# Dense gates of an expert mixer: three bf16 products for one float32 product, and other products in the warm-up

## Chip, core and metric

One core of one Trainium2 chip runs the whole program. The metric is device time in microseconds (us), the median of three runs.

## What is computed

A decoder trunk of two layers over 256 tokens of width 1024, all float32. Each layer has an attention mixer and then an expert mixer; a last RMSNorm ends it. The change lies in the expert mixer, which the reference computes so (cut; 16384 experts are the pairs of 128 first and 128 second indices, 8 heads pick 16 each):

```
q = (t @ w_query).reshape(T, PEER_HEADS, 2, PEER_HALF)
s = jnp.einsum('thpd,pnd->thpn', q, sub_keys)
top_s, top_i = lax.top_k(s, PEER_TOPK)
...
experts = jnp.take_along_axis(cand_i, best_pos, axis=-1).reshape(T, PEER_HEADS * PEER_TOPK)
gates = jax.nn.softmax(best_s, axis=-1).reshape(T, PEER_HEADS * PEER_TOPK)
...
act = jax.nn.gelu(jnp.einsum('td,ted->te', tb, expert_u[eb]), approximate=False)
out = jnp.einsum('te,ted->td', gb * act, expert_v[eb])
```

## The kernel before

The kernel gathers no experts. It multiplies the tokens by all rows of `expert_u` and sums over all rows of `expert_v`, with gates that are zero where an expert was not picked. Weights come in blocks of 128 x 1024 float32, in the order of use; each is split into two float32r parts, `hi` by ScalarE (ACT, L90) and `lo` by VectorE (DVE, L91), up to two blocks ahead, and every product of such operands is three matmuls on TensorE (PE): high by high, high by low, low by high (L119 to L121 for 256 columns, L152 for 512). SP issues the loads (L110).

The program runs layer by layer: the norm (`inv_rms`, `norm_t`), the mixer, the norm again, then `peer`. In `peer` 16 blocks give the queries and their scores; `select` finds the picked pairs and their gates on DVE while the first 48 chunks of `expert_u` are multiplied (a chunk is one of 128 blocks, that is one second index; 24 matmuls of 256 columns). At its end the indices and the gates are transposed to `tT`, with the pick along the partitions and the token along the columns (L942 on PE, L945 on ACT).

Then comes the dense stage: 65 rounds, b = 0 to 64, over blocks of four tokens (`TB`), with the last 80 chunks spread over them. A round with one chunk is called short here, one with two long. A round does, in the order written by hand and kept on each engine:

- `one_hots(b+1)`: DVE compares a table of indices, `iotax`, with the tokens' picks, for the first and the second index: two bf16 tiles [pick, index, token] (L761);
- `proj`: the next chunk (with the split of a later block on ACT and DVE);
- `gated(b+1)`: ACT scales the second index's rows by the gate, token by token, into float32 `ohG` (L770), and copies the first's into float32 `oh` (L771);
- `apply(b-1)`: DVE multiplies the finished chunks by the gates of block b-1 (L786, L788), ACT stores the gates for the later ones (L790);
- `dense(b)`: for each of the four tokens one float32 product of [pick, first index] and [pick, gated second index], 128 x 128, into PSUM (L779);
- for the chunk, ACT's gelu (L743, L745) and DVE's product with gates already stored (L747).

After it, 128 blocks of `expert_v` follow with 12 matmuls of 512 columns each (L152).

At the start PE runs 14 float32 products of a tile `ones` (L285) until the tokens are there. The norm's squares on ACT (L214) write their unused results over `hT[0]`; a diagonal with the reciprocal root (L243) then transposes and scales the tokens on PE (L246), and ACT and DVE cut the result into `hT[0]` and `hT[1]` (L251, L252).

Of the kernel before, what the change touches and what calls it, by code (L numbers as in the profile page):

```python
# [22 lines left out]
S = 256  # L23
# [12 lines left out]
WARM = 14  # L36
# [9 lines left out]
class Kern:  # L46
# [26 lines left out]
    def weights(self, *key):  # L73
        """The two float32r parts of the next block."""
        n = self.used
        self.used += 1
        assert self.blocks[n][0] == key, (self.blocks[n][0], key)
        self.ahead(n + 3)
        return self.split[n]

    def ahead(self, n):
        """Splits blocks up to the n-th and fetches more."""
        nc = self.nc
        while len(self.split) < min(n, self.limit, len(self.blocks)):
            if len(self.raws) == len(self.split):
                self.fetch()
            raw, w = self.raws[len(self.split)]
            hi = self.ring(self.stream, "hi", [128, D + 8], F32R, 3)
            lo = self.ring(self.stream, "lo", [128, D + 8], F32R, 3)
            nc.scalar.activation(hi[:, :w], raw[:, :w], AF.Copy)  # L90
            nc.vector.tensor_sub(lo[:, :w], raw[:, :w], hi[:, :w].bitcast(F32))  # L91
            self.split.append((hi, lo))
        while len(self.raws) < min(len(self.split) + RAWS, len(self.blocks)):
            self.fetch()
# [28 lines left out]
    def proj(self, *key, tag="ps"):  # L123
        """[128 columns, tokens] of h times a block of weights."""
        w = self.by_k(self.weights(*key))
        ps = self.bank(tag)[:, :S]
        self.mm3(ps, [((w[0][:, k], w[1][:, k]), (self.hT[0][:, k], self.hT[1][:, k])) for k in KO])
        return ps

    def ring(self, pool, name, shape, dtype, n):  # L130
        """The next of n tiles that take turns."""
        key = (id(pool), name, *shape)
        if key not in self.rings:
            self.rings[key] = [[pool.tile(shape, dtype, name=f"{name}{q}") for q in range(n)], 0, pool]
        r = self.rings[key]
        while True:
            r[1] += 1
            t = r[0][(r[1] - 1) % n]
            if not any(t is h for h in self.held):
                return t  # L140
# [4 lines left out]
    def rows_b(self, accs, lhs, w, tt, width, first, last):  # L145
        """accs[g] += lhs^T rows (128 of the contraction) times a natural block of weights."""
        hi, lo = w
        lh = lhs[0][..., tt * 128:(tt + 1) * 128]
        ll = lhs[1][..., tt * 128:(tt + 1) * 128]
        for n, (a, b) in enumerate(((lh, hi), (lh, lo), (ll, hi))):  # L150
            for g, ps in enumerate(accs):
                self.nc.tensor.matmul(ps[:, :width], a, b[:, g * width:(g + 1) * width],  # L152
                                      start=first and n == 0, stop=last and n == 2)

    def sum_b(self, n, key, lhs_of):
        """x += sum of n blocks; the last blocks run piece by piece of the result, so that the norm starts early."""
# [26 lines left out]
    def rsqrt_end(self, pool, vy):  # L183
        """One Newton step on the power, in two parts; gives -2 / sqrt."""
# [12 lines left out]
    def inv_rms(self, also=lambda n: None):  # L197
        """Generator: finishes the sums into x; gives -2 / rms of the rows of the first tile of tokens, then of the
        second; also(n) goes with the n-th piece."""
# [35 lines left out]
    def norm_t(self, pool, g):  # L235
        """hT = transpose of the normed x, as two float32r parts; g: the gains [128, KT]. The transposing product
        with a diagonal applies 1 / rms."""
# [18 lines left out]
    def build(self):  # L256
        nc, tc, i = self.nc, self.tc, self.i
        with ExitStack() as st:
# [21 lines left out]
            # the tensor engine's clock rises with work: it runs on ones until x is there  # L280
            ones = const.tile([128, 128], F32, name="ones")
            nc.vector.memset(ones, 1.0)
            ps = self.bank("ps")
            for _ in range(WARM):
                nc.tensor.matmul(ps[:, 0:128], ones, ones, start=True, stop=True)  # L285
            self.iotab = const.tile([128, TOPK], BF, name="iotab")
            self.iotax = const.tile([128, 128, TB], BF, name="iotax")
            self.starts = const.tile([128, 2, 16], BF, name="starts")
# [27 lines left out]
    def constants(self, pool):  # L316
        """Generator, in three steps: the bias by distance (negated) and the mask, over all pairs of tokens, into DRAM."""
# [23 lines left out]
        # the rows run against the distance: read them upside down, turn them with a permutation  # L341
# [12 lines left out]
    def mixer(self, l):  # L354
        nc, tc, i = self.nc, self.tc, self.i
        lam_init = 0.8 - 0.6 * math.exp(-0.3 * l)
        with tc.tile_pool(name="mix", bufs=1) as mp, tc.tile_pool(name="att", bufs=1) as ap, ExitStack() as first:
            self.norm_t(ap, self.gains[:, 0, l])
            # small operands
# [15 lines left out]
            # values and forget logits  # L375
# [26 lines left out]
            # operands of the forgetting scores: even heads in rows 0..63 with their decay in rows 64..79,  # L402
            # odd heads in rows 64..127 with their decay in rows 0..15
# [56 lines left out]
            # branch projections, merge  # L460
# [41 lines left out]
    def forget(self, mp, psv, bf, tri, sel, fq, fk):  # L502
        """Generator, in eight steps: decay operands of the forgetting heads."""
# [8 lines left out]
        # -log_sigmoid(z) = max(-z, 0) + log1p(exp(-|z|))  # L512
# [30 lines left out]
    def exps(self, ap, ps, tb, sums):  # L543
        """exp of the logits less their maximum, both tiles of queries; ps holds the negated scores, tb the
        negated bias."""
# [13 lines left out]
    def turn(self, ap, w):  # L559
        """Transposed weights as blocks (keys 0, queries 0), (keys 0, queries 1), (keys 1, queries 1)."""  # L560
        nc = self.nc
        pt = self.bank("ps")
        for q in range(3):
            nc.tensor.transpose(pt[:, q * 128:(q + 1) * 128], w[:, q * 128:(q + 1) * 128], self.ident)  # L564
        wt = self.ring(ap, "wt", [128, 384], F32, 3)
        nc.scalar.activation(wt, pt[:, 0:384], AF.Copy)
        return wt

    def diff_head(self, ap, h, qk, tb, nlam, dv, ydT, gsub):
        """Generator, in seven steps of one block of weights each: a differential head."""  # L570
# [51 lines left out]
    def fox_pair(self, ap, c, fq, fk, tb, dv, yfT):  # L622
        """Generator, in four steps: two forgetting heads."""
# [34 lines left out]
    def peer(self, l):  # L658
        nc, tc, i = self.nc, self.tc, self.i
        with ExitStack() as st:  # L660
            sm = st.enter_context(tc.tile_pool(name="sm", bufs=1))
            pa = st.enter_context(tc.tile_pool(name="bufa", bufs=1))
            tT = [sm.tile([128, S], F32 if q == 2 else BF, name=f"tT{q}") for q in range(3)]
# [51 lines left out]
            with tc.tile_pool(name="wp", bufs=1) as wp:  # L715
                # dense gates, token by token, against the chunks so far; the later chunks take them as they come
# [37 lines left out]
    def one_hots(self, sm, b, tT):  # L754
        """Rows of the first and of the second index for some tokens, [index, token]."""
# [3 lines left out]
        o = [self.ring(sm, "ohb", shp, BF, 2) for _ in range(2)]  # L759
# [4 lines left out]
    def gated(self, sm, b, tT, hot):  # L764
        """The rows token by token in float32, those of the second index scaled by the gates."""
        nc = self.nc
        oa = self.ring(sm, "oh", [128, TB, 128], F32, 2)
        og = self.ring(sm, "ohG", [128, TB, 128], F32, 2)
        for t in range(TB):
            nc.scalar.activation(og[:, t], hot[1][:, :, t], AF.Copy, scale=tT[2][:, b * TB + t:b * TB + t + 1])  # L770
        nc.scalar.activation(oa, hot[0].rearrange("p n t -> p t n"), AF.Copy)  # L771
        return oa, og

    def dense(self, hots):
        """Gates of all experts [first index, second index] for some tokens."""
        oa, og = hots
        ps = self.bank("acc").rearrange("p (t c) -> p t c", c=128)
        for t in range(TB):
            self.nc.tensor.matmul(ps[:, t], oa[:, t], og[:, t], start=True, stop=True)  # L779
# [12 lines left out]
    def score(self, tk, sk, q, u):  # L792
        """Scores of one half-head against its sub-keys."""
# [8 lines left out]
    def top16(self, tk, items, tag):  # L802
        """Generator: the largest 16 of each list, in order, and their places; the lists take turns."""
# [14 lines left out]
    def select(self, tk, tT):  # L818
        """Best 16 of each half-head, best 16 sums of each head, their experts and gates; yields the time
        that each piece takes on the vector engine, in microseconds, or None to let the other engines catch up."""  # L820
# [29 lines left out]
        # gates; places and index lists as bf16 (whole numbers below 128)  # L850
# [14 lines left out]
        by_h = lambda t: t.rearrange("p (h k) r -> p h k r", h=PH)  # noqa: E731  # L865
# [23 lines left out]
        # row of the candidates: as many as start at or before the place; column: the place less the row's start  # L889
# [15 lines left out]
        # first index: sum of the steps up to the row  # L905
# [17 lines left out]
        # second index: the one at the column  # L923
# [14 lines left out]
        for tt in both:  # L938
# [5 lines left out]
            for q in range(3):  # L944
                nc.scalar.activation(tT[q][:, tt * 128:(tt + 1) * 128], ps[:, q * 128:(q + 1) * 128], AF.Copy)  # L945


def lay_out(inputs, depth=2):
    """Inputs as the kernel reads them: rearranged, never changed."""
# [26 lines left out]
def shape_constants():  # L976
# [9 lines left out]
    # row p < 8 carries ones against the keys' sums, rows 8..15 the queries' sums against ones  # L986
# [11 lines left out]
    # bucket of distance 255 - n; the last row is the mask  # L998
# [27 lines left out]
```

## Time and profile before

| what | value |
|---|---|
| median of three runs | 2064.69 us (2063.64 to 2064.99) |
| profiled execution, first to last instruction (its span; the page gives no other time for it) | 2062.4 us |
| mean granted clock of TensorE | 0.999 of full |
| PE, DVE, ACT busy | 99%, 66%, 63% of the span |

The profile shows one execution. Matmuls are pipelined and their ends are modelled, so a listed duration reaches into the next matmul; distances between starts tell the rate. A weight load (PEld) overlaps the matmul before it. A float32 matmul of the program appears as two records.

### The profile page before, as it was taken

To read this page: it belongs to the slowest core of one execution; us is meant where nothing else is said; L and a number is where in the kernel's file an instruction comes from. 1 tells how busy PE (TensorE), PEld (TensorE's weight loads), DVE (VectorE), ACT (ScalarE), POOL (GpSimd) and SP (SyncE) were. 2 spreads that over 40 slices of the span, in tenths; PEclk is the share of its full clock that TensorE was granted. 3 is DMA by queue.
4 is the path that set the end of the run, shared out by engine and by line. 5 is a ranking of instruction groups with operands and counts; after the bars stand their busy time and mean duration, and the time that the engine had idled before them with its cause. 6 is when DMAs were issued, how large, how long until landed. Compare 5 with 4: busy or idle time off the path is not lost.

```text
span 2062.4 us, 36624 instructions
## 1 busy us (share of the span) xinstructions
PE 2046.8 (99%) x14052; PEld 1888.7 (92%) x14052; DVE 1363.1 (66%) x2990; ACT 1290.6 (63%) x2600; POOL 28.0 (1%) x50
## 2 busy tenths in 40 slices
PE   9999999999999999999999999999999999999998
PEld 8998999999999888888899989999999998888886
DVE  5667798666677555555566668985666775555555
ACT  6666446688888444444466655467888874444444
POOL 2000000000000000000010000000000000000000
PEclk9999999999999999999999999999999999999999
DMA  7445565544444555656554455665444546565654
GB/s 229 148 154 167 164 184 177 181 149 149 148 150 148 182 192 186 192 186 192 186 171 146 157 172 159 190 187 171 145 154 144 152 145 193 186 192 186 191 185 153
DMA packets 97392, 352.72 MB, mean 171 GB/s; under 512 B 11152, under 2 KB 11317, under 8 KB 97216
## 3 DMA queue, kind: packets, MB, share of 16 engines
q1 hardware_dynamic: 95472, 345.68, 53.9%
q0 software_dynamic: 1456, 4.18, 0.7%
q8 instruction: 110, 1.80, 0.4%
q14 instruction: 66, 0.54, 0.1%
q10 hardware_dynamic: 288, 0.52, 0.1%
HBM read 348.62 MB, written 1.71 MB: 170 GB/s over the span
## 4 chain that ended last, share of the span: by engine, by line
PE 98%; issue 1%; DMA 0%; POOL 0%; DVE 0%; ACT 0%; POOLq 0%; SPq 0%
PE acc L152 37%; PE ps L120 17%; PE ps L119 17%; PE ps L121 17%; PE acc L779 6%; PE ps L152 1%; PE acc L797 1%; PE acc L246 1%; PE acc L634 1%; PE ps L564 0%; PE acc L576 0%; DMA tr<-erow 0%; PE acc L651 0%; DMA x<-x 0%; PE acc L120 0%
## 5 line engine op out<-in xcount | busy, mean ns | idle before, releaser
L91 DVE TENSOR_TENSOR lo<-raw,hi 128x1024 fp32r<-128x1024 f32 (+1 forms) x656 | 801.9, 1224 | 497.9 <-ACT hi L90 493.4
L90 ACT ACTIVATE hi<-raw 128x1024 fp32r<-128x1024 f32 (+1 forms) x656 | 694.8, 1060 | 395.3 <-PE acc L152 387.9
L119 PE MATMUL ps<-hT,hi 128*128 128x256 f32 x2784 | 799.6, 287 | 0.0
L120 PE MATMUL ps<-hT,hi 128*128 128x256 f32 x2784 | 784.5, 282 | 0.0
L121 PE MATMUL ps<-hT,lo 128*128 128x256 f32 x2784 | 779.0, 280 | 0.0
L152 PE MATMUL acc<-hi,cut 128*128 128x512 f32 x2048 | 561.1, 395 | 0.0
L119 PEld LDWEIGHTS ps<-hT,hi 128*128 128x128 f32 x2784 | 523.4, 188 | 3.9 <-issue 3.7
L121 PEld LDWEIGHTS ps<-hT,lo 128*128 128x128 f32 x2784 | 525.1, 189 | 0.0
L120 PEld LDWEIGHTS ps<-hT,hi 128*128 128x128 f32 x2784 | 523.6, 188 | 0.3
L152 PEld LDWEIGHTS acc<-hi,cut 128*128 128x128 f32 x2048 | 385.4, 188 | 90.0
L152 PE MATMUL acc<-lo,cut 128*128 128x512 f32 x1024 | 321.9, 394 | 0.0
L152 PEld LDWEIGHTS acc<-lo,cut 128*128 128x128 f32 x1024 | 192.4, 188 | 45.8
L770 ACT ACTIVATE ohG<-ohb,tT 128x128 f32<-128x128 bf16 x512 | 168.6, 404 | 5.4 <-DVE ohb L761 2.2
L779 PE MATMUL acc<-ohG,oh 128*128 128x128 f32 x1024 | 134.7, 274 | 0.0
L747 DVE TENSOR_TENSOR bufb<-bufb,g 128x4 f32<-128x4 f32 (+25 forms) x156 | 45.9, 294 | 124.0 <-ACT g L743 124.0
L779 PEld LDWEIGHTS acc<-ohG,oh 128*128 128x128 f32 x1024 | 125.2, 191 | 0.0
L682 ACT ACTIVATE bufa<-ps 128x256 f32<-128x256 f32 x96 | 36.9, 384 | 115.7 <-PE ps L121 115.6
L761 DVE TENSOR_TENSOR ohb<-iotax,tT 128x512 bf16<-128x512 bf16 x256 | 96.5, 419 | 3.8 <-ACT oh L771 3.8
L743 ACT ACTIVATE g<-ps 128x4 f32<-128x4 f32 (+25 forms) x156 | 43.1, 276 | 75.5 <-PE ps L121 73.6
L771 ACT ACTIVATE oh<-ohb 128x512 f32<-128x512 bf16 x128 | 85.0, 664 | 0.0
L708 DVE TENSOR_TENSOR cut<-bufb,cut 128x256 fp32r<-128x256 f32 x160 | 67.1, 419 | 0.0
L707 ACT ACTIVATE cut<-bufb 128x256 fp32r<-128x256 f32 x160 | 64.0, 400 | 0.0
(235 smaller groups left out, 1442.8 us busy)
## 6 DMA issues: line engine op xcount, KB each, us to landing
raw<-uT SPq DMA_DIRECT2D x256, 512.0 KB, 3.5
raw<-expert_v SPq DMA_DIRECT2D x256, 512.0 KB, 4.3
raw<-wA SPq DMA_DIRECT2D x64, 512.0 KB, 3.7
raw<-wQ SPq DMA_DIRECT2D x32, 512.0 KB, 3.6
raw<-wV SPq DMA_DIRECT2D x16, 516.0 KB, 4.5
raw<-wO SPq DMA_DIRECT2D x16, 512.0 KB, 3.7
raw<-w_out SPq DMA_DIRECT2D x16, 512.0 KB, 4.3
tb<-table POOLq DMA_DIRECT2D x2, 640.0 KB, 5.6
```

Of the source, the lines that this page charges most:

```text
L90: nc.scalar.activation(hi[:, :w], raw[:, :w], AF.Copy)
L91: nc.vector.tensor_sub(lo[:, :w], raw[:, :w], hi[:, :w].bitcast(F32))
L119: self.nc.tensor.matmul(ps, ah, bh, start=first and q == 0, stop=False)
L120: self.nc.tensor.matmul(ps, ah, bl, start=False, stop=False)
L121: self.nc.tensor.matmul(ps, al, bh, start=False, stop=last and q == n - 1)
L152: self.nc.tensor.matmul(ps[:, :width], a, b[:, g * width:(g + 1) * width], start=first and n == 0, stop=last and n == 2)
L707: nc.scalar.activation(a[:, 0], chunk(n), AF.Copy)
L708: nc.vector.tensor_sub(a[:, 1], chunk(n), a[:, 0].bitcast(F32))
L761: nc.vector.tensor_tensor(o[q], self.iotax, tT[q][:, None, ts].to_broadcast(shp), op=OP.is_equal)
L770: nc.scalar.activation(og[:, t], hot[1][:, :, t], AF.Copy, scale=tT[2][:, b * TB + t:b * TB + t + 1])
L771: nc.scalar.activation(oa, hot[0].rearrange("p n t -> p t n"), AF.Copy)
L779: self.nc.tensor.matmul(ps[:, t], oa[:, t], og[:, t], start=True, stop=True)
```

## The change

The gates are no longer float32 in `tT[2]`. `select` cuts them into three bf16 parts, each the rounding of what the parts before leave, so that their sum is the gate exactly; the tile `gp` holds them [pick, part, token]. `gated` is now one DVE multiplication of the second index's one-hots with the three parts, into a bf16 tile [pick, part, index, token]; the first index's one-hots go to PE as they are, in a ring of two tiles (the second's have one). `dense` does three bf16 products per token into the same PSUM region. PE reads both operands with a step of four elements, since the token is the innermost dimension. ACT has no part in `gated` any more.

The warm-up is seven kinds of products, five times each: bf16 with 512, 128, 128 (both operands with a step of four) and 384 columns, float32r with 512, 512 (step of two) and 128 columns. The bf16 ones read `iotax`, set to ones; the float32r ones read the first half of `hT[0]`, set to ones. The tile `ones` is gone. The rest of the diff (left out) takes comments away.

```diff
-WARM = 14
+WARM = 5
...
-            ones = const.tile([128, 128], F32, name="ones")
-            nc.vector.memset(ones, 1.0)
-            ps = self.bank("ps")
-            for _ in range(WARM):
-                nc.tensor.matmul(ps[:, 0:128], ones, ones, start=True, stop=True)
             self.iotab = const.tile([128, TOPK], BF, name="iotab")
             self.iotax = const.tile([128, 128, TB], BF, name="iotax")
+            ones = self.hT[0][:, 0:4].rearrange("p k t -> p (k t)")
+            nc.vector.memset(self.iotax, 1.0)
+            nc.vector.memset(ones.bitcast(F32), 1.0)
+            ps = self.bank("ps")
+            onesb = self.iotax.rearrange("p n t -> p (n t)")
+            for a, b, n in ((onesb, onesb, 512), (onesb, onesb, 128), (self.iotax[:, :, 0], self.iotax[:, :, 1], 128),
+                            (onesb, onesb, 384), (ones, ones, 512), (ones, ones[:, ::2], 512), (ones, ones, 128)):
+                for _ in range(WARM):
+                    nc.tensor.matmul(ps[:, :n], a[:, 0:128], b[:, :n], start=True, stop=True)
...
-            tT = [sm.tile([128, S], F32 if q == 2 else BF, name=f"tT{q}") for q in range(3)]
+            tT = [sm.tile([128, S], BF, name=f"tT{q}") for q in range(2)] + [sm.tile([128, 3, S], BF, name="gp")]
...
-        o = [self.ring(sm, "ohb", shp, BF, 2) for _ in range(2)]
+        o = [self.ring(sm, f"oh{q}", shp, BF, 2 - q) for q in range(2)]
...
     def gated(self, sm, b, tT, hot):
-        nc = self.nc
-        oa = self.ring(sm, "oh", [128, TB, 128], F32, 2)
-        og = self.ring(sm, "ohG", [128, TB, 128], F32, 2)
-        for t in range(TB):
-            nc.scalar.activation(og[:, t], hot[1][:, :, t], AF.Copy, scale=tT[2][:, b * TB + t:b * TB + t + 1])
-        nc.scalar.activation(oa, hot[0].rearrange("p n t -> p t n"), AF.Copy)
-        return oa, og
+        og = self.ring(sm, "ohG", [128, 3, 128, TB], BF, 2)
+        shp = [128, 3, 128, TB]
+        self.nc.vector.tensor_tensor(og, hot[1][:, None].to_broadcast(shp),
+                                     tT[2][:, :, None, b * TB:(b + 1) * TB].to_broadcast(shp), op=OP.mult)
+        return hot[0], og
...
         for t in range(TB):
-            self.nc.tensor.matmul(ps[:, t], oa[:, t], og[:, t], start=True, stop=True)
+            for k in range(3):
+                self.nc.tensor.matmul(ps[:, t], oa[:, :, t], og[:, k, :, t], start=k == 0, stop=k == 2)
...
-            for q in range(3):
-                nc.scalar.activation(tT[q][:, tt * 128:(tt + 1) * 128], ps[:, q * 128:(q + 1) * 128], AF.Copy)
+            ts = slice(tt * 128, (tt + 1) * 128)
+            for q in range(2):
+                nc.scalar.activation(tT[q][:, ts], ps[:, q * 128:(q + 1) * 128], AF.Copy)
+            rest = self.ring(tk, "rest", [128, 128], F32, 2)
+            nc.scalar.activation(tT[2][:, 0, ts], ps[:, 256:384], AF.Copy)
+            nc.vector.tensor_sub(rest, ps[:, 256:384], tT[2][:, 0, ts])
+            nc.scalar.activation(tT[2][:, 1, ts], rest, AF.Copy)
+            nc.vector.tensor_sub(tT[2][:, 2, ts], rest, tT[2][:, 1, ts])
```

## Rows read from the trace of the kernel before

**Rows 1.** The page, busy time, share and instructions of each engine

```profile
PE 2046.8 (99%) x14052; PEld 1888.7 (92%) x14052; DVE 1363.1 (66%) x2990; ACT 1290.6 (63%) x2600; POOL 28.0 (1%) x50
```

**Rows 2.** The page, chain that ended last, shares by engine

```profile
PE 98%; issue 1%; DMA 0%; POOL 0%; DVE 0%; ACT 0%; POOLq 0%; SPq 0%
```

**Rows 3.** The same chain in order of time: start, length, engine, tile, line

```profile
395.08 0.89 PE acc L779 x8
401.65 0.89 PE acc L779 x8
405.37 0.89 PE acc L779 x8
```

**Rows 4.** Timeline of ACT, two chunks before the dense stage: start, length

```profile
386.62 0.38 ACT L682 ACTIVATE bufa<-ps 128x256 f32<-128x256 f32 x1 [0.99 <-PE ps L121]
...
389.45 0.38 ACT L682 ACTIVATE bufa<-ps 128x256 f32<-128x256 f32 x1 [1.49 <-PE ps L121]
```

**Rows 5.** Timeline of ACT, two blocks of expert_v

```profile
840.74 1.06 ACT L90 ACTIVATE hi<-raw 128x1024 fp32r<-128x1024 f32 x1 [1.41 <-PE acc L152]
...
843.53 1.06 ACT L90 ACTIVATE hi<-raw 128x1024 fp32r<-128x1024 f32 x1 [1.43 <-PE acc L152]
```

**Rows 6.** Window: PE, PEld, DVE, ACT, POOL busy, granted clock, DMA

```profile
394.00:672.00 278.00, 278.00 (x2384) 278.00 (x2383) 191.93 (x407) 236.16 (x612) 0.00 (x0) 1.00 0.49 150
```

**Rows 7.** Groups of weight loads, shapes apart: busy us, mean ns

```profile
L120 PEld LDWEIGHTS ps<-hT,hi 128*128 128x128 f32 x2784 | 523.6, 188 | 0.3
...
L564 PEld LDWEIGHTS ps<-ident,lg 128*128 128x128 f32 x48 | 5.4, 140 | 0.0
...
L333 PEld LDWEIGHTS acc<-oh,rel 33*5 33x5 f32 x2 | 0.1, 82 | 0.2 <-issue 0.2
```

**Rows 8.** Groups of ACT and DVE, shapes apart

```profile
L770 ACT ACTIVATE ohG<-ohb,tT 128x128 f32<-128x128 bf16 x512 | 168.6, 404 | 5.4 <-DVE ohb L761 2.2
...
L761 DVE TENSOR_TENSOR ohb<-iotax,tT 128x512 bf16<-128x512 bf16 x256 | 96.5, 419 | 3.8 <-ACT oh L771 3.8
...
L891 DVE TENSOR_TENSOR cmp<-wide,starts 128x2048 bf16<-128x2048 bf16 x4 | 4.7, 1219 | 0.0
```

**Rows 9.** Timeline of DVE, a short round of the dense stage

```profile
523.44 0.28 DVE L747 TENSOR_TENSOR bufb<-bufb,g 128x116 f32<-128x116 f32 x1 [0.77 <-ACT g L743]
523.63 0.75 DVE L761 TENSOR_TENSOR ohb<-iotax,tT 128x512 bf16<-128x512 bf16 x2
524.56 1.22 DVE L91 TENSOR_TENSOR lo<-raw,hi 128x1024 fp32r<-128x1024 f32 x1 [0.17 <-ACT hi L90]
525.71 0.35 DVE L786 TENSOR_TENSOR bufa<-acc,bufa 128x192 f32<-128x192 f32 x1
525.97 0.30 DVE L788 TENSOR_TENSOR bufb<-acc,bufb 128x148 f32<-128x148 f32 x1
```

**Rows 10.** Timeline of DVE at the end of the selection

```profile
382.50 1.23 DVE L91 TENSOR_TENSOR lo<-raw,hi 128x1024 fp32r<-128x1024 f32 x1 [2.43 <-ACT hi L90]
```

**Rows 11.** Timeline of the start

```profile
0.86 0.17 DVE L282 MEMSET ones<- 128x128 f32 x1
...
1.08 4.93 PE L285 MATMUL ps<-ones 128*128 128x128 f32 x28 [1.08 <-DVE ones L282]
...
3.42 0.63 ACT L214 ACTIVATE hT<-x 128x512 fp32r<-128x512 f32 x1 [1.40 <-DMA x<-x]
...
7.08 0.29 DVE L243 TENSOR_SCALAR diag<-ident,rs_y 128x128 f32<-128x128 f32 x1 [0.97 <-DMA ident<-c_ident]
...
7.42 3.86 PE L246 MATMUL acc<-diag,x 128*128 128x128 f32 x32 [1.41 <-DVE diag L243]
...
10.53 1.55 ACT L251 ACTIVATE hT<-acc,gains 128x256 fp32r<-128x256 f32 x4
```

**Rows 12.** Windows of the warm-up: length, PE busy, clock, DMA

```profile
1.67:4.23 2.56, 2.56 (x13) 1.00 0.81 261
4.39:5.74 1.35, 1.35 (x15) 1.00 0.97 310
```

## The prediction

> **What bounds the kernel now.** I read the page's busy table first: TensorE (PE) is busy 99% of the span, VectorE (DVE) 66% [rows 1]. A busy PE need not be at its peak, so next the chain that ended last: 98% of it is PE's [rows 2]. Followed in order of time, the dense products stand in it one burst per four tokens, eight passes in 0.89 us [rows 3]. So in the stage that the change touches, PE's own issue rate sets the time, and what an instruction costs there is the distance to the next start, not its listed duration. Three such distances. A chunk without dense work (24 float32r products of 256 columns) takes 389.45 - 386.62 = 2.83 us, 118 ns a product [rows 4]. A block of the second half (12 products of 512 columns) takes 843.53 - 840.74 = 2.79 us, 232 ns a product [rows 5]. A float32 pass of 128 columns takes 0.89 / 8 = 111 ns [rows 3]; a float32 product is two of them. In all three every product has its own weight load, and the load shows nowhere: it runs below the product before it. The window over the first layer's dense stage agrees: PE 278 of 278 us, ScalarE (ACT) 236, DVE 192 [rows 6].
>
> **The dense products.** Removed: 1024 float32 passes (2 layers x 64 blocks x 4 tokens x 2). Each block takes 0.895 us of PE (0.89 in the chain, and 3.72 less 2.83 from burst to burst), 128 blocks 114.6 us. Added: 1536 bf16 products of 128 columns, 12 a block, each with a load of 128 bf16 columns. No row of before has a bf16 product, so it is bounded. From above by the nearest row, the float32 pass with the same 128 x 128 shape: 111.5 ns. From below: that pass spends 111.5 ns on 128 columns, float32r spends 118 ns on 256, so a column goes in at least twice as fast, 55.8 ns for 128. The line through the float32r points (256 columns 118 ns, 512 columns 232 ns) gives 61 ns at 128 columns; 118 / 2 gives 59. I take 60, because float32r too is done in one pass, as bf16 is. Block: 12 x 60 = 0.72 us. Gain (0.895 - 0.72) x 128 = 22.4 us. The bounds: 0.67 us (gain 28.8) and 1.338 us (loss 56.7).
>
> Whether a load fits below a product of 60 ns is the open point. A load of 5 float32 columns takes 82 ns and one of 128 takes 188 [rows 7]: 106 / 123 = 0.86 ns a column, 110 ns for 128, just covered by 111 and 118 ns. The transposes' load of 128 columns takes 140 ns, so 58 / 123 = 0.47 ns a column, 60 ns for 128: the array can be filled at this rate, even from 4-byte values. I put bf16, half the bytes, with this row, and the load is then just covered by its product.
>
> **The rows by token.** Removed from ACT: 512 scalings of 404 ns [rows 8] and 128 copies of the other rows. They lay beside PE (ACT has 42 us free in the 278 of the stage [rows 6]), so nothing comes back from them. Added on DVE: 128 products of bf16 with 1536 elements. DVE takes 419 ns for 512 bf16 elements and 1219 for 2048 [rows 8], 0.52 ns an element, both with a broadcast operand: 0.95 us for 1536. At the end of one instruction the next has already started some 0.085 us before, so it adds 0.865 us. For a block with one chunk the starts [rows 9] give 0.19 (product with g) + 0.67 (one-hots) + 1.15 (split) + 0.26 + 0.22 (gates into both buffers) = 2.49 us; with the new product 3.36, against PE's 2.83 + 0.72 = 3.55. A block with two chunks has 4.7 against 6.38. DVE is covered, with 0.2 us to spare in short blocks; the late ones, with wider gate products, use it up and recover in the long ones (80 chunks in 65 rounds, so 15 of them). In its queue behind the new product stand the gates' application and the product with g, and PE waits for neither for over a block. The new wait (one-hots wait until the dense burst two blocks earlier has released its operand) is over when the application, which waits for the same burst, can run. Cost 0; without this cover, the third rival below.
>
> **The end of the selection.** One ACT copy and two DVE subtractions more for each half of the tokens, in a chain of some 0.6 us. ACT's next weight split stands behind them, and DVE's behind that; it waits 2.43 us for ACT there already [rows 10], and the block is needed two chunks (5.7 us) after its buffer came free. Hidden.
>
> **The warm-up.** Removed: 28 float32 passes, 1.08 to 6.01 us [rows 11]. Added: 35 products, 5 x 2304 = 11520 columns. The clock column reads full speed for both, but 13 passes touch 2.56 us early on and 15 touch 1.35 us after 4.39 us [rows 12]: a pass takes 0.21 us, then 0.11, so PE runs at 1.2 GHz, and at 2.4 after some 3.2 us of work. The first filling of 512 elements may take 0.5 us by the 0.17 us for 128 [rows 11], so PE starts at 1.35 us. Until 4.5 us it does 3.15 x 1200 = 3800 columns, then 7700 at 0.455 ns = 3.5 us: it ends at 8.0, its last result at 8.2. The operand of the float32r part is now the first half of hT, and the first squares of the norm are written over it: they start at 8.2, not at 3.42. After that the steps keep their distances of before (square to first diagonal 7.08 - 0.97 - 3.42 = 2.7 us without the wait for the identity, from there 0.34 to PE), and PE transposes the second tile behind the first, 16 passes each: 8.2 + 2.7 + 0.34 + 16 x 0.112 = 13.0; 0.65 us later ScalarE takes the first pair of blocks, at 13.7 instead of 10.53. I take +3.2 us; PE leads from there to the end, so it stays. Bounds: +0.7 (squares not held; PE's own end at 8.1 against 7.42) and +5.9 (all 11520 columns at 1.2 GHz, end at 10.9).
>
> **Sum.** -22.4 + 3.2 = -19.2 us. The page gives only the span for the profiled execution, 2062.4, so 2043.2 after. The runs' median lies 2.3 us above the span, which I leave: 2064.69 - 19.2 = 2045.5.
>
> **Rivals.** *1, the load or the stride binds (slower).* If bf16 columns are loaded at the float32 rate of 0.86 ns, or the operands' step of four elements costs a second cycle a column, a product takes 111.5 ns, a block 1.338 us: +56.7 + 3.2, 2124.6 us. For it: 2784 x 3 float32r loads all take 188 ns, at no better rate, and PE reads no operand with a step in this kernel. Against it: the 140 ns load. It decides from 72.5 ns a product on ((114.6 - 3.2) / 1536).
> *2, the load sticks out in part.* With so short a product a third to a half of the 60 ns of filling may lie open: 75 to 90 ns a product, at 82.5 a block of 0.99 us, +12.2 + 3.2: 2080. For it: 256-column products still pay 118 where the 512-column slope alone gives 114. Against it: loads and products overlap fully in each row so far.
> The Trainium skill ("TensorE: Matmul & The Clock Gate", Back-to-back issue gap) speaks for this one: it says that in a stream of load and product pairs 128 columns cost about 81 ns each, which would make a block 0.97 us and the kernel 13 us slower, 2078. The same place has 131 ns for 512 columns, and this trace has 232 [rows 5], so I don't follow its figure.
> *3, DVE becomes the bound.* If the new product runs at one element a cycle, the float32 rate (1.22 us for 1024 elements, 0.35 for 192 [rows 9], so 1.76 for 1536), a short block takes 4.17 us and a long one 5.5: 49 short and 15 long ones 287 us a layer, against 3.72 and 6.57 now [rows 3], 281: +12 + 3.2: 2080. Against it: both bf16 rows run at twice that rate.
>
> **How the numbers follow.** A run of this kernel can tell about 0.2%, 4.1 us, from no change. The forecast has 0.60, its own range 2036 (55.8 ns, warm-up +0.7) to 2057 (66 ns, +5.9). A price between 66 and 74 ns, 0.05, ends within 0.2%. Rival 1 has 0.17, rival 2 0.15, rival 3 0.03, all slower. So faster 0.60, same 0.05, slower 0.35. The range goes from 2036 to 2085, which takes in rival 3 and rival 2 up to 86 ns, and leaves out rival 1 and the rest of rival 2.
>
> **What would show it.** Starts of dense bursts 3.55 us apart in short blocks (3.72 now); a burst of 12 in 0.72 us; PE full in the whole stage, with no wait on DVE; the first square near 8.2 us, the first transposes near 11; ACT far below 236 in the stage. A burst of 1.3 us is rival 1, one of 1.0 rival 2, PE waiting on the gated rows rival 3. I am wrong above all if a bf16 pair costs more than 72 ns.

## The result and the profile after

The changed kernel takes 2139.49 us (2139.04 to 2140.36), the kernel before 2064.58 us (four executions, one more than in the table above): a ratio of 1.0364, interval 1.0349 to 1.0379. It is slower by 75 us, where 19 us faster was forecast and 2036 to 2085 us was the range. The span of the profiled execution is 2137.4 us, 75.0 more than before.

The page of the changed kernel, busy time, share and instructions of each engine, against [rows 1]:

```profile
PE 2120.6 (99%) x14571; PEld 1951.1 (91%) x14571; DVE 1477.2 (69%) x3127; ACT 1061.0 (50%) x1964; POOL 28.1 (1%) x50
```

The chain that ended last in order of time, against [rows 3] (start, length):

```profile
402.08 1.43 PE acc L782 x12
409.17 1.42 PE acc L782 x12
413.43 1.42 PE acc L782 x12
```

and two of its groups of instructions (busy us, mean ns of one):

```profile
L782 PEld LDWEIGHTS <-oh 128*128 128x128 bf16 x1536 | 163.4, 118 | 7.8
L772 DVE TENSOR_TENSOR ohG<-oh,gp 128x1536 bf16<-128x1536 bf16 x128 | 121.8, 952 | 0.1
```

The move of the work is as planned: ACT 230 us less busy, DVE 114 more, the new DVE product 952 ns. But a dense burst, the products of one block of four tokens, has become longer, 1.42 us where it was 0.89 us. That is 1.42 / 12 = 118 ns a bf16 product. Long rounds last 409.17 - 402.08 = 7.09 us (6.57 before), short ones 413.43 - 409.17 = 4.26 us (3.72). PE is still without a gap: busy 250 of 250 us from 410 to 660.

The first dense burst starts 402.08 - 395.08 = 7.0 us later than before. The other 68.0 us of the span are the 128 bursts, 0.53 us each.

The 7.0 us arise at the start, where the first product with weights begins 8.0 us later than before (19.03 us for 11.04); 1.0 us of that is made up again before the first dense burst. Lines of the timeline there, against [rows 11] (start, length, engine):

```profile
2.31 0.15 PEld L291 LDWEIGHTS <-iotax 128*128 128x128 bf16 x1 [0.28 <-issue]
...
2.74 0.15 PEld L291 LDWEIGHTS <-iotax 128*128 128x128 bf16 x1 [0.28 <-issue]
...
5.33 0.15 PEld L291 LDWEIGHTS <-iotax 128*128 128x128 bf16 x1 [0.17 <-issue]
5.65 0.15 PEld L291 LDWEIGHTS <-iotax 128*128 128x128 bf16 x1 [0.17 <-issue]
...
6.04 4.70 PE L291 MATMUL ps<-hT 128*128 128x512 f32 x15
8.23 0.21 PEld L291 LDWEIGHTS ps<-hT 128*128 128x128 f32 x1 [0.26 <-issue]
8.70 0.21 PEld L291 LDWEIGHTS ps<-hT 128*128 128x128 f32 x1 [0.26 <-issue]
...
10.78 0.63 ACT L214 ACTIVATE hT<-x 128x512 fp32r<-128x512 f32 x1 [5.94 <-PE ps L291]
...
13.83 5.45 PE L246 MATMUL acc<-diag,x 128*128 128x128 f32 x32 [3.09 <-DVE diag L243]
...
18.02 3.29 ACT L251 ACTIVATE hT<-acc,gains 128x256 fp32r<-128x256 f32 x8 [2.78 <-issue]
```

The squares stand behind PE's last read of `hT[0]`, at 10.78 instead of 3.42 us. A float32r product of 512 columns with a step of two takes 8.70 - 8.23 = 0.47 us (0.45 to 0.47 for the five), twice the 0.23 us of [rows 5]. The transposes last 5.45 us instead of 3.86. The windows (length, busy time of PE, PEld, DVE, ACT, POOL, granted clock, DMA) say why:

```profile
13.80:17.20 3.40, 3.37 (x16) 3.37 (x17) 2.66 (x6) 1.45 (x2) 3.22 (x7) 0.50 0.11 12
17.20:20.00 2.80, 2.80 (x24) 2.80 (x24) 1.86 (x5) 1.98 (x5) 2.13 (x4) 0.99 0.91 188
```

PE had waited 3.09 us for the diagonal; the granted clock then was half, 1.2 GHz, for the next 3.4 us.

### The profile page after: what moved, and what is told of

It is laid out like the page before. It is cut to its first block, busy times and chain, and to the rows that moved or that the text cites. A ratio compares the mean times of both kernels' runs of the same rounds, so it can differ in the third digit from the quotient of the medians.

```text
span 2137.4 us, 37154 instructions
## 1 busy us (share of the span) xinstructions
PE 2120.6 (99%) x14571; PEld 1951.1 (91%) x14571; DVE 1477.2 (69%) x3127; ACT 1061.0 (50%) x1964; POOL 28.1 (1%) x50
## 4 chain that ended last, share of the span: by engine, by line
PE 97%; issue 1%; DMA 0%; DVE 0%; POOL 0%; ACT 0%; POOLq 0%; ACTq 0%
PE acc L152 36%; PE ps L120 16%; PE ps L119 16%; PE ps L121 16%; PE acc L782 9%; PE ps L152 1%; PE acc L800 1%; PE acc L246 0%; PE acc L638 0%; PE ps L568 0%; PE acc L580 0%; DMA tr<-erow 0%; DMA lam<-diff_lambda 0%; PE acc L655 0%; PE acc L120 0%
## 5 line engine op out<-in xcount | busy, mean ns | idle before, releaser
L793 ACT ACTIVATE bufb<-acc 128x312 f32<-128x312 f32 (+42 forms) x128 | 38.8, 303 | 341.6 <-DVE bufb L791 282.7
L782 PE MATMUL acc<-ohG,oh 128*128 128x128 bf16 x1536 | 202.6, 296 | 0.0
L782 PEld LDWEIGHTS <-oh 128*128 128x128 bf16 x1536 | 163.4, 118 | 7.8
L772 DVE TENSOR_TENSOR ohG<-oh,gp 128x1536 bf16<-128x1536 bf16 x128 | 121.8, 952 | 0.1
L765 DVE TENSOR_TENSOR oh<-iotax,tT 128x512 bf16<-128x512 bf16 x256 | 96.5, 418 | 0.0
```

Source lines behind the costliest of these rows:

```text
L765: nc.vector.tensor_tensor(o[q], self.iotax, tT[q][:, None, ts].to_broadcast(shp), op=OP.is_equal)
L772: self.nc.vector.tensor_tensor(og, hot[1][:, None].to_broadcast(shp), tT[2][:, :, None, b * TB:(b + 1) * TB].to_broadcast(shp), op=OP.mult)
L782: self.nc.tensor.matmul(ps[:, t], oa[:, :, t], og[:, k, :, t], start=k == 0, stop=k == 2)
```

## The experiments

Three theories of a product's 118 ns: A, the step of the moving operand (the gated rows, whose columns PE streams through the array); B, the step of the weights (the first index's one-hots, loaded ahead of each product); C, the load of bf16 weights as such. A fourth, L, a loop between DVE and ACT, came up with the second of these experiments. Where one time stands without a range, the kernel was executed once; the kernel before took 2063.8 to 2064.1 us beside each.

**Seven kinds of products by themselves.** In place of the warm-up's loop, after 40 float32r products:

```diff
+            for _ in range(24):
+                nc.tensor.matmul(ps[:, :128], onesb[:, 0:128], onesb[:, 0:128], start=True, stop=True)
+            for _ in range(24):
+                nc.tensor.matmul(ps[:, :128], onesb[:, 0:256:2], onesb[:, 0:128], start=True, stop=True)
...
+            for _ in range(24):
+                nc.tensor.matmul(ps[:, :128], onesb[:, 0:512:4], onesb[:, 0:512:4], start=True, stop=True)
```

> The changed kernel with another warm-up: 40 float32r products of 512 columns to bring the clock up, then seven kinds of bf16 products of 128 columns, 24 of each, one line each; the step of the weights and of the moving operand (in elements) is 1/1, 2/1, 4/1, 1/2, 1/4, 2/2, 4/4. The price of a kind is the distance from its first start to the next kind's, over 24. Theory A, the moving operand's step binds (a column 8 bytes further on costs 0.91 ns, 4 bytes are free): 56 to 62 ns for all kinds with moving step 1 or 2, 117 ns for 1/4 and 4/4. Theory B, the step in the weights binds: 117 ns for 4/1 and 4/4, about 60 for 1/4. Theory C, a load of 128 bf16 weights takes over 100 ns however it lies: 107 to 117 ns for all seven.

PE in its timeline, the seven kinds in the order of the text above:

```profile
14.03 1.51 PE L291 MATMUL ps<-iotax 128*128 128x128 bf16 x24
15.38 1.50 PE L293 MATMUL ps<-iotax 128*128 128x128 bf16 x24
16.72 1.50 PE L295 MATMUL ps<-iotax 128*128 128x128 bf16 x24
18.06 1.55 PE L297 MATMUL ps<-iotax 128*128 128x128 bf16 x24
19.45 2.94 PE L299 MATMUL ps<-iotax 128*128 128x128 bf16 x24
22.21 1.56 PE L301 MATMUL ps<-iotax 128*128 128x128 bf16 x24
23.61 2.99 PE L303 MATMUL ps<-iotax 128*128 128x128 bf16 x24
26.42 3.75 PE L246 MATMUL acc<-diag,x 128*128 128x128 f32 x32
```

The starts give 56 ns without a step ((15.38 - 14.03) / 24), 56 with weights of step two and 56 with step four; 58 with a moving step of two, 115 with one of four; 58 for two and two, and 117 for four and four. A bf16 element has 2 bytes, so steps of two and four elements are 4 and 8 bytes. So A is right for the price: 8 bytes from column to column of the moving operand double it, 4 bytes cost 2 ns, the weights' step costs nothing beside a moving operand without a step (56 ns) and 2 ns beside one of four (117 against 115), and the load of 128 bf16 weights fits below a product of 56 ns. The granted clock was 1.00 from 14 to 30 us. B and C fall. That bytes count and not elements agrees with the float32r product above, where a step of two is 8 bytes and doubles the price too. The run's own time, 2151.1 us, has the longer warm-up in it.

The Trainium skill ("SBUF — State Buffer", Door 1: The DMA port swizzle, on cache lines) says that full bandwidth needs at least two accesses to each line of 16 bytes. Steps of 8 bytes make two, and the product still takes twice as long; four accesses, at a step of 4 bytes, do it. The Trainium skill ("TensorE: Matmul & The Clock Gate", Weight-path perf modes) allows packed or strided weights for its fast load, and the 56 ns with stepped weights agree with that.

**Contiguous operands in the dense stage.** The tiles stay as they are; only what PE reads changes. The gates come out mixed up, so these three runs tell times and nothing else (shown: the moving operand alone):

```diff
+        oc = oa.rearrange("p n t -> p (n t)")
+        gc = og.rearrange("p k n t -> p k (n t)")
...
-                self.nc.tensor.matmul(ps[:, t], oa[:, :, t], og[:, k, :, t], start=k == 0, stop=k == 2)
+                self.nc.tensor.matmul(ps[:, t], oa[:, :, t], gc[:, k, t * 128:(t + 1) * 128], start=k == 0, stop=k == 2)
```

> PE reads the gated rows as contiguous runs of 128 elements of the same tile, so the moving operand has no step and the weights keep theirs; the gates that come out are mixed up, everything else is as in the changed kernel. A: bursts of 12 in 0.72 us, 3.55 us between bursts in short rounds, the kernel 0.69 x 128 = 88 us faster than the changed one, near 2051 us. B and C: 4.26 us between bursts, no change, 2139 us.

> The other half alone: the weights are read as contiguous runs, the moving operand keeps its step of four; the gates are mixed up here too. A and C: 4.26 us between bursts in short rounds, 2139 us. B: 3.55 us, near 2051 us.

> Both operands read as contiguous runs, with mixed-up gates. A: as with the moving operand alone, near 2051 us. B: as with the weights alone, near 2051 us. If each step binds by itself, only this one is fast and the two before stay at 2139 us. C: 2139 us.

Measured: moving operand 2118.8 us, weights 2135.0, both 2119.7. Without the weights' step a product costs (2139.5 - 2135.0) / 1536 = 2.9 ns less, about the table's 2. Removing the moving step helps, but by 21 us instead of 88: A, right for the price, missed this one, and so did B and C. The timeline of the run with the contiguous moving operand, PE's bursts and DVE and ACT of one short round:

```profile
536.85 0.83 PE L784 MATMUL acc<-ohG,oh 128*128 128x128 bf16 x12 [0.52 <-DVE ohG L772]
...
541.16 0.83 PE L784 MATMUL acc<-ohG,oh 128*128 128x128 bf16 x12 [0.60 <-DVE ohG L772]
...
541.28 0.30 DVE L793 TENSOR_TENSOR bufb<-acc,bufb 128x144 f32<-128x144 f32 x1
...
541.68 0.32 ACT L795 ACTIVATE bufb<-acc 128x176 f32<-128x176 f32 x1 [2.71 <-DVE bufb L793]
541.89 0.26 ACT L747 ACTIVATE g<-ps 128x116 f32<-128x116 f32 x1
...
542.19 0.28 DVE L751 TENSOR_TENSOR bufb<-bufb,g 128x116 f32<-128x116 f32 x1 [0.60 <-ACT g L747]
...
542.38 0.75 DVE L765 TENSOR_TENSOR oh<-iotax,tT 128x512 bf16<-128x512 bf16 x2
543.31 1.22 DVE L91 TENSOR_TENSOR lo<-raw,hi 128x1024 fp32r<-128x1024 f32 x1 [0.18 <-ACT hi L90]
544.46 0.95 DVE L772 TENSOR_TENSOR ohG<-oh,gp 128x1536 bf16<-128x1536 bf16 x1
545.33 0.35 DVE L791 TENSOR_TENSOR bufa<-acc,bufa 128x192 f32<-128x192 f32 x1
545.59 0.30 DVE L793 TENSOR_TENSOR bufb<-acc,bufb 128x148 f32<-128x148 f32 x1
```

The burst is short now (0.83 us with its drain), but it waits for DVE's gated rows, and the bursts are 541.16 - 536.85 = 4.31 us apart. No engine is full (of the 250 us from 410 to 660 PE is busy 234, DVE 201, ACT 101). DVE's product into `bufb` (541.28) releases ACT's store of the later gates (541.68), which waited 2.71 us for it although the two write different parts of `bufb`; behind the store, in ACT's queue, stands the gelu (541.89), and DVE waits 0.60 us for that before its product with g (542.19). From there DVE's own queue leads through one-hots, split, gated rows and application to the next product into `bufb` at 545.59: 4.31 us round. This is theory L. As an estimate, the same loop without DVE's new product (545.33 - 544.46 = 0.87 us) would be 3.44 us, below PE's 3.72 of before.

**A step of two, and the loop cut.** Tokens by pairs, so that PE's step is two elements, 4 bytes; the rest as in the change (cut: the table of indices and the gates' parts, laid out by pairs too):

```diff
-        shp = [128, 128, TB]
+        shp = [128, 2, 128, 2]
...
-        og = self.ring(sm, "ohG", [128, 3, 128, TB], BF, 2)
-        shp = [128, 3, 128, TB]
...
+        og = self.ring(sm, "ohG", [128, 2, 3, 128, 2], BF, 2)
+        shp = [128, 2, 3, 128, 2]
+        gate = tT[2][:, b * 2:(b + 1) * 2, :, None]
+        self.nc.vector.tensor_tensor(og, hot[1][:, :, None].to_broadcast(shp), gate.to_broadcast(shp), op=OP.mult)
...
-                self.nc.tensor.matmul(ps[:, t], oa[:, :, t], og[:, k, :, t], start=k == 0, stop=k == 2)
+                self.nc.tensor.matmul(ps[:, t], oa[:, t // 2, :, t % 2], og[:, t // 2, k, :, t % 2], start=k == 0, stop=k == 2)
```

> Tokens interleaved by two instead of four, for one-hots, gate parts and gated rows, so PE reads both operands with a step of 4 bytes; the gates come out right. The price of a product falls from 117 to 58 ns (first run's kind 2/2). Theory L, a loop that goes from the gates' application on DVE to ACT's store of the later gates, from there to ACT's gelu of the chunk, to DVE's product with g, and through DVE's queue back to the application, takes 4.3 us a short round: bursts 4.2 to 4.3 us apart in short rounds although PE needs only 3.5, with PE waiting on DVE's gated rows, near 2119 us as in the run with contiguous moving operand. Theory A alone (only the operand's step binds): 3.53 us apart, 2139.5 - 0.72 x 128 = 2047 us.

Then, in `apply`, ACT's store ahead of DVE's products:

```diff
+        if J < NJ:
+            nc.scalar.activation(bufb[:, J - M_PRE:, ts], pv[:, J:], AF.Copy)
         nc.vector.tensor_mul(bufa[:, :, ts], pv[:, :M_PRE], bufa[:, :, ts])
         if J > M_PRE:
             nc.vector.tensor_mul(bufb[:, :J - M_PRE, ts], pv[:, M_PRE:J], bufb[:, :J - M_PRE, ts])
-        if J < NJ:
-            nc.scalar.activation(bufb[:, J - M_PRE:, ts], pv[:, J:], AF.Copy)
```

> The run by pairs, and in the gates' application ACT's store of the later gates is issued ahead of DVE's products, so that it waits for nothing that DVE does in this round. L: the loop is cut, DVE has 3.36 to 3.5 us of work a short round, PE leads again: bursts 3.53 us apart, no wait of PE on the gated rows, near 2047 us. Rival, DVE's own work is what binds: bursts stay above 4 us apart, near 2110 to 2119 us.

The pairs alone take 2117.7 us, with PE waiting 0.50 and 0.57 us for the gated rows before bursts; with the store ahead 2053.0 us, 65 us less, and no such wait. L holds, and DVE's own work is not what bound. The time is 6 us above the 2047 expected, about what rounds of 3.59 us instead of 3.53 make in 128.

The loop costs in short rounds alone. In the run by pairs they are 3.6 us apart up to the eighth burst, as with the loop cut, and 3.9 to 4.7 us from there; long rounds are 6.4 us in both runs. From the first to the last burst of a layer that makes 297.3 us against 268.7, so 57 us for both layers. The other 7 to 8 us lie elsewhere and were not followed up.

> The changed kernel (step of four, new warm-up) with ACT's store ahead of DVE's products, nothing else. If PE's price of 117 ns a product sets the time of the changed kernel and the loop lies just below it: 4.25 us between bursts as before, 2139 us, at most 2 us less. If the loop sets it: up to 20 us less.

2140.2 us, bursts 4.26 us apart: with the step of four PE's price alone sets the changed kernel, and the loop of about the same length beside it adds nothing. (At the start of this run the granted clock was 0.50 for 6.8 us instead of 3.4, and the first product with weights came 0.6 us later.)

> The kernel before with the same two statements swapped. If the gain of the swap comes from cutting a loop that needs DVE's new product to get long (without it 4.3 - 0.87 = 3.4 us, against PE's 3.72): no change, 2064 us. If the order is better in itself: 2055 us or less.

2063.7 us against 2064.0: the order is worth nothing while the loop is short.

**The start.** One character, `self.hT[1]` for `self.hT[0]` under the warm-up's float32r part:

> The changed kernel, with the float32r part of its warm-up reading hT[1], over which no square is written. If the squares held behind the warm-up (and the clock that fell behind their wait) make most of the 7 us at the start: squares from 3.4 us on, transposes right after the warm-up's end at 10.6 us at full clock, the first product of the layer at about 14.4 us instead of 19.0, the kernel 4.6 us faster, 2135 us. If the warm-up's own length makes it: the first product stays near 19 us and the time at 2139.5.

2133.4 us, 6.1 less. Its timeline:

```profile
3.42 0.63 ACT L214 ACTIVATE hT<-x 128x512 fp32r<-128x512 f32 x1 [1.40 <-DMA x<-x]
...
5.41 4.23 PE L291 MATMUL ps<-hT 128*128 128x512 f32 x15
...
9.48 3.79 PE L246 MATMUL acc<-diag,x 128*128 128x128 f32 x32
12.02 3.28 ACT L251 ACTIVATE hT<-acc,gains 128x256 fp32r<-128x256 f32 x8 [1.63 <-PE acc L246]
```

The squares are back at 3.42, and the transposes follow the warm-up directly, in 3.79 us. ACT cuts the result from 12.02 on, 6.0 us earlier than at 18.02. Of these, 3.1 are PE's wait for the diagonal and 1.7 the slower transposes (5.45 against 3.79 us): the hold and the fall of the clock behind it. The remaining 1.2 us is the warm-up itself, whose float32r part starts at 5.41 instead of 6.04 and lasts 4.23 us instead of 4.70. Products of 384 columns start 0.16 us apart here from 4.9 us on, where they were 0.32 us apart (5.65 - 5.33). So the clock rose earlier, with the same products before it; why is open. The expected 4.6 us had the warm-up end at 10.6 us as before.

The old warm-up in the changed kernel:

```diff
+            ones = const.tile([128, 128], F32, name="ones")
+            nc.vector.memset(ones, 1.0)
+            ps = self.bank("ps")
+            for _ in range(14):
+                nc.tensor.matmul(ps[:, 0:128], ones, ones, start=True, stop=True)
```

> The changed kernel with the 14 float32 products on a tile of their own as warm-up, as before. If dense stage and warm-up add up, it gives back what the first dense burst comes late by, 7.0 us: 2132.5 us, the first burst at 394.9 us as before. If the later start is made up or doubled further on: nearer 2139.5 or below 2130.

2132.2 us (2131.7 to 2132.5), so 7.3 us less, the 2132.5 expected: the two parts of the change add up.

**All three.** Pairs, store ahead, old warm-up:

> Pairs of tokens, ACT's store ahead of DVE's products, and the old warm-up together. The run by pairs with the store ahead took 2053.0 us; the old warm-up gave the changed kernel back 7.3 us. If the three parts add up: 2045.7 us, 0.9% below the kernel before. If the early start is lost again in the dense stage or the loads of the weights: nearer 2053.

2046.35 us (2045.0 to 2047.6), a ratio to the kernel before of 0.9915, interval 0.9901 to 0.9928. That is 0.9% faster than the kernel before, near the 2045.7 expected. Its chain in order of time:

```profile
401.34 0.71 PE acc L780 x12
404.93 0.71 PE acc L780 x12
```

and its window over the first dense stage, against [rows 6]:

```profile
394.00:660.00 266.00, 266.00 (x2603) 263.14 (x2602) 234.45 (x463) 119.10 (x291) 0.00 (x0) 1.00 0.51 155
```

Short rounds take 3.59 us, PE is full, DVE busy 234 of 266 us. A burst and what follows it take 3.59 - 2.83 = 0.76 us, 0.13 less than before; by 128, 17 us, the measured 17.7. Of the 0.76, 0.70 are the products (12 x 58 ns). The remaining 0.06 us may be the first float32r load, which needs more than the 58 ns of the last product; that is argued, not shown.

## Why the prediction was wrong, step by step

**The price of a product failed.** The step of the prediction was: "I take 60, because float32r too is done in one pass, as bf16 is." It took 118 ns in the kernel, and the 8-byte step of the moving operand was the cause, by the table: 115 ns for that step alone, 56 without. The question was put to the load, where the conclusion was right: with no step, each load is covered by a product of 56 ns. The step stood in the text only as the second half of rival 1, "the operands' step of four elements costs a second cycle a column", with the objection against rival 1 (the 140 ns load) speaking to its first half only. The outcome of that half is what came, at 0.53 us x 128 = 68 us where 0.443 x 128 = 56.7 had been its price.

**"DVE is covered, with 0.2 us to spare in short blocks" failed too,** hidden behind the first. DVE's own 3.36 us fit (with pairs and the store ahead it keeps up with rounds of 3.59 us), but the sum left out that DVE's queue leads through ACT: application, ACT's store, gelu, product with g. That loop takes 4.31 us. Its last link stood in the rows that were summed: DVE waits 0.77 us there for ACT's gelu [rows 9], and a sum of DVE's own work has no place for it. With the price of 60 ns that was forecast, the kernel would still have been slower than before, near 2118 us, as the run by pairs shows (58 ns a product). So the forecast had two independent faults, and either alone ends above its range: the loop 2117.7 us, the price, with the loop cut, 2140.2.

**The rival with a third to a half of the load lying open** fell: 56 ns a pair. Rival 3's mechanism, DVE at one element a cycle, fell too: 952 ns for 1536 elements instead of 1.76 us. The Trainium skill ("TensorE: Matmul & The Clock Gate", Back-to-back issue gap) has 81 ns for such a pair of load and product; the 56 ns measured do not agree with it.

**The warm-up** was right in kind and short in size: +3.2 forecast, bounds 0.7 to 5.9, measured +7.0 in the first burst and 7.3 in time. The hold of the squares came as described, but at 10.78 instead of 8.2, for two reasons. The early products ran at half rate for longer than the 4.5 us that were assumed: 384 columns still take 0.32 us at 5.33, and 512 float32r columns take 0.23 us from 7.1 us on. (The granted-clock column reads 1.00 there, as it does in [rows 12]; the distances tell the rate.) And the five float32r products with a step took 0.47 us instead of 0.23, some 1.1 us in all. The squares at 10.78 still lie within the upper bound, which had the warm-up end at 10.9; what that bound lacked was the fall of the clock behind PE's wait for the diagonal: transposes of 5.45 us instead of 3.86.

**Right:** ACT's relief brought nothing to the path, the end of the selection stayed hidden (the first burst is late by no more than the start is), the new DVE product took 0.95 us, and the sum's own logic, that PE's issue distances set the stage, held in the changed kernel.

## What to carry to other kernels

Before a product is made cheaper by type, look at the step of its moving operand: here 8 bytes from column to column doubled the price and 4 bytes cost 2 ns of 58, and interleaving tokens by two instead of four left DVE's product as fast as it was (951 ns against 952). And when work moves to an engine that has room, add up not its own queue but the loop through every engine that it waits for in a round; an in-order queue with one early wait (ACT's store) can turn 3.4 us of DVE's work into a round of 4.3. And a warm-up should not hold a tile that the first real work writes.

## What the runs showed that was not expected

The price of a stepped product did not follow the clock. With 8-byte steps a bf16 product of 128 columns takes 115 to 118 ns at 2.4 GHz, twice a contiguous one. In the changed kernel's warm-up the five stepped products start 118 ns apart (from 4.13 to 4.72 us) at half rate too, where the contiguous ones just before them start 107 ns apart. So the step does not cost "a second cycle a column" of PE's clock, as rival 1 put it; at the slow clock it costs 11 ns of 118. What sets the 118 ns was not tested. The step of the weights costs at most 3 ns of 117. After 3.1 us without work PE's granted clock read 0.50 for 3.4 us; with 1.4 us of waiting at the same place before, it had stayed at 1.00.
